# The step sizes' logarithm in the decay exponents, and a predicated copy between the two directions

## The chip, the cores and the metric

The kernel runs on one core of one Trainium2 chip. The metric is the device time of one execution in microseconds (us). A core has TensorE for matrix products (PE in the rows; its weight loads are PEld), VectorE (DVE), ScalarE (ACT), GpSimd (POOL), and SyncE (SP), whose queue issues the DMA transfers. Each engine runs its own queue in order; semaphores tie the queues together.

## The reference, cut to what matters

The model is a two-layer encoder over 512 tokens of width 1024. Layer 0 mixes tokens by retention and neighbourhood attention, layer 1 by a bidirectional state space scan; each layer ends in a gated feed-forward block. The change touches only the state space mixer of layer 1: 32 heads of width 64 in 4 groups of 8 heads, each direction with step sizes dt and decays of its own.

```python
dt = softplus(dt_raw.reshape(bsz, s, 2, SSD_HEADS) + dt_bias)
log_a = dt * -exp(a_log)
v_f = xh * dt[:, :, 0];  v_b = xh * dt[:, :, 1]
y = bidir_scan(qc, kb, v_f, v_b, log_a[:, :, 0], log_a[:, :, 1])
# within one chunk of 128 tokens and one direction:
seg = cs[:, :, None] - cs[:, None, :]            # cs = cumsum(log_a)
decay = exp(where(mask, seg, -inf))
y_intra = einsum('bjlgh,blghp->bjghp', qk[..., None] * decay, vv)   # vv = x * dt
```

Within a chunk, token j therefore gets from token l the product qk(j,l) times exp(cs(j) - cs(l)) times dt(l) times x(l), by the forward quantities where l <= j and by the backward ones elsewhere.

## The kernel before, in words

The trunk runs `mixer0`, `ffn`, `mixer1`, `ffn` in that order. Every projection is done in split precision: `mm3` (lines 86 to 88) issues three matrix products for one, on high and low parts that `split` makes (ACT cast at line 81, DVE subtraction at line 82). Weights come in 512 KB units through `wunit`, whose DMA (line 61) goes into one of three buffers `wst`.

`mixer1` first runs `steps` (lines 588 to 652). It computes dt for all 64 direction-heads over 512 tokens as 128 x 256 tiles, the running sums `pf`, the scalings `ysc` (to DRAM as `yd`) and `sw`, writes `pf` to DRAM as `pd`, and turns three tiles by PE transposes into `tok`, a token-major tile with 128 tokens on the partitions: `tok[:, 0]` holds the running sums, `tok[:, 1]` dt, `tok[:, 2]` sw. Line 652 makes `ddt`, the difference of the two directions' dt.

After that each group goes through a list of named tasks written out by hand (`SLOTS`): "t" and "n" are projections of this and the next group, "G" the 4 products of B and C per group (`gt`), "s" the chunk states, "h" one head's decay matrix, "i" the contribution of the states for a pair of heads, "p" the matrix products of a pair of heads (`py`, line 782), "r" and "o" the normalisation and output projection of the group before. This list gives the program order. The framework's scheduler then sets the order in each engine's queue when the kernel is built: by program order, by what it reckons ready, with the weight splits moved ahead by `high_priority(60)`. So a queue is not in program order throughout; but once built, it is fixed.

One head (`head`, lines 729 to 747) loads two rows of `pd`, one for each direction, broadcast to all 128 partitions (`pb`, 256 KB each, 3 buffers, line 736). Then, for each of 4 chunks, ACT computes tok minus pb for the forward direction (line 741), DVE takes the backward difference and the larger of the two (line 742), and ACT computes `ds`, which is dt forward where the mask `um` is one and dt backward elsewhere (line 744). Over the whole 128 x 512 tile follow one exponential on ACT (745), the product with `gt` on DVE (746) and the product with `ds` on DVE (747). The result is waited for by `pair`, whose 16 matrix products of a pair of heads all wait for both heads. `state` (line 717) multiplies x by rows of `tok[:, 2]`.

Of the kernel before, what the change touches and what calls it, by code (L numbers as in the profile page):

```python
# [7 lines left out]
F32 = mybir.dt.float32  # L8
R32 = mybir.dt.float32r
BF16 = mybir.dt.bfloat16  # L10
AF = mybir.ActivationFunctionType
ALU = mybir.AluOpType
PSUM = bass.MemoryType.PSUM
# [2 lines left out]
P = 128  # L16
S = 512
NT = S // P
# [517 lines left out]
SSD_H = NG * HPG  # L536
# [16 lines left out]
def mixer1(E, w_dt, w_fm, cw, dtc, cols, mask, w_out, g_post_row, done):  # L553
# [4 lines left out]
    nc, tc = E.nc, E.tc  # L558
    C = P
    H, H2 = SSD_H, 2 * SSD_H  # L560
    with ExitStack() as ctx:
        pool = lambda name, bufs: ctx.enter_context(tc.tile_pool(name=name, bufs=bufs))
        one, two, four = pool("m1", 1), pool("m1b", 2), pool("m1d", 4)
# [14 lines left out]
            nc.sync.dma_start(xd[t], E.x[:, t, :])  # L578


        tok = one.tile([P, 3, NT, H2], F32, name="tok")
        ddt = one.tile([P, NT, H], F32, name="ddt")
        etot = one.tile([P, H2, NT], F32, name="etot")
        pd = E.dram.tile([H2, S], F32, name="pd")
        yd = E.dram.tile([H2, S], F32, name="yd")
# [1 line left out]
        def steps():  # L587

            st = E.wst.tile([P, 512], F32, name="wst")
            nc.sync.dma_start(st, w_dt)  # L590
            wh = E.whi.tile([P, 512], R32, name="whi")
            wl = E.wlo.tile([P, 512], R32, name="wlo")
            E.split(wh, wl, st)
            ps = E.mm.tile([P, S], F32, name="mm")
            for k in range(KD):
                c = slice(k * H2, k * H2 + H2)
                E.mm3(ps[:H2], wh[:, c], wl[:, c], E.xh[:, k], E.xl[:, k], k == 0, k == KD - 1)
            bc = few.tile([P, 2], F32, name="bc")
            nc.sync.dma_start(bc, dtc)
            nc.scalar.activation(bc[:, 1:2], bc[:, 1:2], AF.Exp)  # L600
            nc.vector.tensor_scalar(bc[:, 1:2], bc[:, 1:2], -1.0, None, op0=ALU.mult)
            half = lambda name: E.tmp.tile([P, 256], F32, name=name, tag="tmp")
            chunks = lambda ap: ap.rearrange("p (c l) -> p c l", c=2)
            z, la, pf, tm = half("z"), half("la"), half("pf"), half("tm")
            for i in range(2):
                nc.scalar.activation(z[i * H2:i * H2 + H2], ps[:H2, i * 256:i * 256 + 256], AF.Identity,
                                     bias=bc[:H2, 0:1])
            with tc.tile_pool(name="lp", bufs=1) as lpp:
                dt = lpp.tile([P, 256], F32, name="dt")
                sw = lpp.tile([P, 256], F32, name="sw")  # L610
                ysc = lpp.tile([P, 256], F32, name="ysc")
                msk = half("msk")
                lp = log1p_exp_neg(E, lambda n: lpp.tile([P, 256], F32, name="lp_" + n), z)
                nc.vector.scalar_tensor_tensor(dt, z, 0.0, lp, op0=ALU.max, op1=ALU.add)
                nc.vector.tensor_scalar(la, dt, bc[:, 1:2], None, op0=ALU.mult)
                nc.vector.memset(msk, 1.0)
                nc.vector.memset(chunks(msk)[:, :, 0:1], 0.0)
                nc.vector.tensor_tensor_scan(pf, msk, la, 0.0, op0=ALU.mult, op1=ALU.add)
                ones = lpp.tile([P, P], F32, name="ones")
                diag = lpp.tile([P, 2, P], F32, name="diag")  # L620
                tot = lpp.tile([P, 2, 1], F32, name="tot")
                nc.vector.tensor_copy(tot, chunks(pf)[:, :, C - 1:C])
                for i in range(2):
                    r = slice(i * H2 + H, i * H2 + H2)
                    nc.vector.tensor_tensor(pf[r], pf[r], la[r], op=ALU.subtract)
                nc.vector.tensor_tensor(chunks(tm), tot.broadcast_to([P, 2, C]), chunks(pf), op=ALU.subtract)
                et = lpp.tile([P, 2], F32, name="et")
                nc.scalar.activation(et, tot.rearrange("p c o -> p (c o)"), AF.Exp)

                nc.vector.memset(ones, 1.0)  # L630
                for c in range(2):
                    nc.vector.tensor_scalar(diag[:, c], E.ident, et[:, c:c + 1], None, op0=ALU.mult)
                pe = E.px.tile([P, 2, P], F32, name="pe", tag="px")
                nc.tensor.matmul(pe.rearrange("p c n -> p (c n)"), ones, diag.rearrange("p c n -> p (c n)"),
                                 start=True, stop=True)
                nc.scalar.copy(etot.rearrange("p h (i c) -> p c i h", i=2), pe.rearrange("p c (i h) -> p c i h", i=2))
                for i in range(2):
                    r = slice(i * H2, i * H2 + H2)
                    nc.sync.dma_start(pd[:, i * 256:i * 256 + 256], pf[r])
                    f, b = slice(i * H2, i * H2 + H), slice(i * H2 + H, i * H2 + H2)  # L640
                    nc.scalar.activation(ysc[f], pf[f], AF.Exp)
                    nc.scalar.activation(ysc[b], tm[b], AF.Exp)
                    nc.scalar.activation(sw[f], tm[f], AF.Exp)
                    nc.scalar.activation(sw[b], pf[b], AF.Exp)
                    nc.sync.dma_start(yd[:, i * 256:i * 256 + 256], ysc[r])
                nc.vector.tensor_tensor(sw, sw, dt, op=ALU.mult)
                for i, s in enumerate((pf, dt, sw)):
                    pt = E.px.tile([P, 2, 2, H2], F32, name="pt", tag="px")
                    for c in range(2):
                        nc.tensor.transpose(pt[:, c].rearrange("p i h -> p (i h)"), s[:, c * C:(c + 1) * C], E.ident)  # L650
                    nc.scalar.copy(tok[:, i].rearrange("p (i c) h -> p c i h", i=2), pt)
            nc.vector.tensor_tensor(ddt, tok[:, 1, :, :H], tok[:, 1, :, H:], op=ALU.subtract)

        def rows(i, dr, g, c):
            o = dr * H + g * HPG
            return tok[:, i, c, o:o + HPG].rearrange("p (h o) -> p h o", o=1).broadcast_to([P, HPG, 64])
# [55 lines left out]
        def state(o, dr, i):  # L712

            g = o["g"]
            c = i if dr == 0 else NT - 1 - i
            xs = E.tmp.tile([P, 512], F32, name="xs", tag="tmp")
            nc.vector.tensor_tensor(hv(xs), hv(o["x"][:, c]), rows(2, dr, g, c), op=ALU.mult)
            ps = E.px.tile([P, 512], F32, name="st", tag="px")
            nc.tensor.matmul(ps, o["bt"][:, c], xs, start=True, stop=True)  # L719
            ns = one.tile([P, 512], F32, name=f"state{dr}{i}")  # L720
            if i == 0:
                nc.scalar.copy(ns, ps)
            else:
                h = dr * H + g * HPG
                nc.vector.tensor_tensor(hv(ns), hv(o["st"][dr, i - 1]), etot[:, h:h + HPG, c:c + 1].broadcast_to([P, HPG, 64]),
                                        op=ALU.mult)
                nc.vector.tensor_tensor(ns, ps, ns, op=ALU.add)
            o["st"][dr, i] = ns

        def head(o, j):  # L730

            g = o["g"]
            h = g * HPG + j
            pb = [three.tile([P, S], F32, name="pb", bufs=3) for _ in range(2)]
            for dr in range(2):
                nc.sync.dma_start(pb[dr], pd[dr * H + h].partition_broadcast(P))
            e = three.tile([P, NT, C], F32, name="e")
            ds = ys.tile([P, NT, C], F32, name="ds")
            for c in range(NT):
                cc = slice(c * C, (c + 1) * C)  # L740
                nc.scalar.activation(e[:, c], pb[0][:, cc], AF.Identity, scale=-1.0, bias=tok[:, 0, c, h:h + 1])  # L741
                nc.vector.scalar_tensor_tensor(e[:, c], pb[1][:, cc], tok[:, 0, c, H + h:H + h + 1], e[:, c],
                                               op0=ALU.subtract, op1=ALU.max)
                nc.scalar.activation(ds[:, c], um, AF.Identity, scale=ddt[:, c, h:h + 1], bias=tok[:, 1, c, H + h:H + h + 1])  # L744
            nc.scalar.activation(e, e, AF.Exp, scale=-1.0)
            nc.vector.tensor_tensor(e, e, o["gt"], op=ALU.mult)
            o["m"][j] = e, nc.vector.tensor_tensor(e, e, ds, op=ALU.mult)  # L747

        def inter(o, q):

# [228 lines left out]
def _layouts(np, i):  # L979
# [19 lines left out]
    cw = np.concatenate([i["c_conv_w"][0], i["c_conv_b"][0][None]])  # L999
    xw, bw, cw = cw[:, :2048].reshape(6, NG, 4, P), cw[:, 2048:2560].reshape(6, NG, 1, P), cw[:, 2560:].reshape(6, NG, 1, P)  # L1000
    a["c_cw"] = np.concatenate([bw, cw, xw], 2).transpose(3, 1, 2, 0)
    a["c_dtc"] = np.tile(np.stack([i["c_dt_bias"][0].reshape(-1), i["c_a_log"][0].reshape(-1)], 1), (2, 1))
    d = np.repeat(i["c_d_skip"][0].reshape(4 * NG, 2), 64, 1)
    a["c_cols"] = np.stack([d.T, i["c_norm_g"][0].reshape(4 * NG, P).T], 1)
    a["c_mask"] = np.triu(np.ones((P, P), np.float32))
# [37 lines left out]
```

## Time and profile before

| | us |
|---|---|
| median of 3 runs | 1435.91 |
| lowest, highest | 1434.77, 1436.99 |
| the profiled execution | 1435.64 |
| its span in the trace | 1433.9 |
| PE busy | 1400.5 |
| DVE busy | 945.2 |
| ACT busy | 718.4 |
| POOL busy | 61.4 |

The span is the stretch from the first to the last recorded instruction; 1.7 us of the profiled execution lie around it. Busy time counts the union of an engine's instructions. "Idle before" in the rows is time in which an engine had nothing running just before an instruction, with the event that ended it. PEclk is TensorE's granted clock as a share of full speed (1.0 is 2.4 GHz, 0.5 is 1.2 GHz).

### The profile page before, as it was taken

The page shows a single profiled execution, that of the slowest core. Times are in us where ns is not written, and L with a number is a line of the kernel's source. Part 1 is how long each engine was busy: PE and PEld are TensorE (multiplying, and loading weights), DVE is VectorE, ACT ScalarE, POOL GpSimd, SP SyncE. Part 2 cuts the span into 40 slices and gives each one's busy share as a digit, 9 for nine tenths or more (in the row PEclk, how much of TensorE's full clock was granted, in tenths as well). Part 3 has the DMA queues.
Part 4 walks back from the last instruction along what each step waited for, and adds up shares of the span by engine and source line. Part 5 has one row for each costly group of instructions (what it writes and reads, how often), then busy time and mean ns, then how long its engine had stood idle before and what let it go on. Part 6 is the DMA issues. An engine that isn't in the chain of part 4 may idle for free.

```text
span 1433.9 us, 18004 instructions
## 1 busy us (share of the span) xinstructions
PE 1400.5 (98%) x6832; PEld 1144.0 (80%) x6832; DVE 945.2 (66%) x1486; ACT 718.4 (50%) x1192; POOL 61.4 (4%) x67
## 2 busy tenths in 40 slices
PE   7999999999999999999999999999889999999998
PEld 6877777898888888888778787777678888888886
DVE  6478888666566552457789886998986666564232
ACT  4346666444444431334887866676644444443230
POOL 0010110100000000000000000000110000000000
PEclk9999999999999999999999999999999999999999
DMA  7443232232332333423565354354532333323221
GB/s 283 148 132 101 85 96 77 86 105 89 103 93 99 101 93 100 131 84 107 144 190 172 121 172 142 93 153 154 152 114 83 100 101 91 103 90 102 88 103 59
DMA packets 56950, 166.34 MB, mean 116 GB/s; under 512 B 7200, under 2 KB 7968, under 8 KB 56864
## 3 DMA queue, kind: packets, MB, share of 16 engines
q1 hardware_dynamic: 56864, 165.20, 36.4%
q8 instruction: 54, 0.88, 0.2%
q14 instruction: 32, 0.26, 0.1%
HBM read 157.57 MB, written 5.51 MB: 114 GB/s over the span
## 4 chain that ended last, share of the span: by engine, by line
PE 88%; DVE 4%; ACT 3%; DMA 2%; issue 2%; POOL 0%; SPq 0%; DVEq 0%; POOLq 0%; ACTq 0%
PE mm L86 27%; PE mm L87 26%; PE mm L88 26%; PE pi L762 1%; DMA pb<-pd 1%; PE st L719 1%; PE py L782 1%; PE pt L140 1%; PE y L449 1%; PE sc L433 1%; DVE wlo L82 0%; PE pt L663 0%; PE sc L434 0%; DMA x<-in_x 0%; ACT whi L81 0%
## 5 line engine op out<-in xcount | busy, mean ns | idle before, releaser
L88 PE MATMUL mm<-xl,whi 128*128 128x512 f32 (+2 forms) x1216 | 463.4, 381 | 3.0 <-DVE xl L82 3.0
L86 PE MATMUL mm<-xh,whi 128*128 128x512 f32 (+1 forms) x1216 | 464.5, 382 | 1.4 <-ACT bf L692 1.2
L87 PE MATMUL mm<-xh,wlo 128*128 128x512 f32 (+2 forms) x1216 | 462.8, 381 | 0.0
L82 DVE TENSOR_TENSOR wlo<-wst,whi 128x1024 fp32r<-128x1024 f32 (+1 forms) x208 | 256.0, 1231 | 125.2 <-ACT whi L81 120.6
L81 ACT CAST whi<-wst 128x1024 fp32r<-128x1024 f32 (+1 forms) x208 | 216.5, 1042 | 125.9 <-PE mm L87 96.3
L88 PEld LDWEIGHTS mm<-xl,whi 128*128 128x128 f32 (+1 forms) x1216 | 229.0, 188 | 47.2 <-DVE xl L82 3.2
L86 PEld LDWEIGHTS mm<-xh,whi 128*128 128x128 f32 x1216 | 229.2, 188 | 46.2 <-ACT bf L692 1.6
L87 PEld LDWEIGHTS mm<-xh,wlo 128*128 128x128 f32 (+1 forms) x1216 | 229.0, 188 | 42.7 <-issue 0.6
L227 DVE SCALAR_TENSOR_TENSOR cv<-mm,cwt,cv 128x511 f32<-128x511 f32 x88 | 66.0, 750 | 148.9 <-ACT cv L226 148.9
L226 ACT ACTIVATE cv<-mm,cwt 128x512 f32<-128x512 f32 x88 | 68.7, 780 | 128.0 <-PE mm L88 128.0
L86 PE MATMUL mm<-whi,hh 128*128 128x512 f32 x288 | 112.0, 389 | 0.0
L87 PE MATMUL mm<-whi,hl 128*128 128x512 f32 x288 | 112.0, 389 | 0.0
L88 PE MATMUL mm<-wlo,hh 128*128 128x512 f32 x288 | 112.0, 389 | 0.0
L81 ACT CAST hh<-cv 128x512 fp32r<-128x512 f32 x44 | 27.3, 621 | 103.3 <-DVE cv L235 103.3
L228 DVE SCALAR_TENSOR_TENSOR cv<-mm,cwt,cv 128x511 f32<-128x511 f32 x88 | 66.0, 750 | 3.0
L86 PEld LDWEIGHTS mm<-whi,hh 128*128 128x128 f32 x288 | 54.1, 188 | 11.3
L87 PEld LDWEIGHTS mm<-whi,hl 128*128 128x128 f32 x288 | 54.1, 188 | 11.2
L88 PEld LDWEIGHTS mm<-wlo,hh 128*128 128x128 f32 x288 | 54.1, 188 | 11.2
L744 ACT ACTIVATE ds<-um,tok,ddt 128x128 f32<-128x128 f32 x128 | 55.3, 486 | 11.9 <-DVE e L747 11.8
L741 ACT ACTIVATE e<-pb,tok 128x128 f32<-128x128 f32 x128 | 43.1, 392 | 16.6 <-DMA pb<-pd 14.6
L82 DVE TENSOR_TENSOR hl<-cv,hh 128x512 fp32r<-128x512 f32 x44 | 30.5, 693 | 28.9 <-ACT hh L81 28.9
L683 DVE SCALAR_TENSOR_TENSOR xf<-mm,cwt,xf 128x511 f32<-128x511 f32 (+1 forms) x64 | 47.2, 741 | 3.1 <-ACT xf L680 2.9
(236 smaller groups left out, 1932.8 us busy)
## 6 DMA issues: line engine op xcount, KB each, us to landing
wst<-in_f_up SPq DMA_DIRECT2D x88, 512.0 KB
wst<-in_f_down SPq DMA_DIRECT2D x44, 512.0 KB
wst<-in_c_fm SPq DMA_DIRECT2D x40, 512.0 KB
pb<-pd SPq DMA_DIRECT2D x64, 256.0 KB
wst<-in_ab_fm SPq DMA_DIRECT2D x20, 512.0 KB
gain<-yd SPq DMA_DIRECT2D x32, 256.0 KB
wst<-in_c_out SPq DMA_DIRECT2D x16, 512.0 KB
gain<-in_norms SPq DMA_DIRECT2D x8, 512.0 KB
```

What stands on the lines that cost most here:

```text
L81: self.nc.scalar.copy(hi, src)
L82: self.nc.vector.tensor_tensor(lo, src, hi.bitcast(F32), op=ALU.subtract)
L86: mm(out, lh, rh, start=first, stop=False)
L87: mm(out, ll, rh, start=False, stop=False)
L88: mm(out, lh, rl, start=False, stop=last)
L140: nc.tensor.transpose(pt[:, j], xs[:, j * P:(j + 1) * P], self.ident)
L226: nc.scalar.activation(o, ps, AF.Identity, scale=w(1), bias=w(3))
L227: nc.vector.scalar_tensor_tensor(o[:, 1:], ps[:, :S - 1], w(0), o[:, 1:], op0=ALU.mult, op1=ALU.add)
L228: nc.vector.scalar_tensor_tensor(o[:, :S - 1], ps[:, 1:], w(2), o[:, :S - 1], op0=ALU.mult, op1=ALU.add)
L683: nc.vector.scalar_tensor_tensor(r[:, a], ps[:, b], wc(j), r[:, a], op0=ALU.mult, op1=ALU.add)
L741: nc.scalar.activation(e[:, c], pb[0][:, cc], AF.Identity, scale=-1.0, bias=tok[:, 0, c, h:h + 1])
L744: nc.scalar.activation(ds[:, c], um, AF.Identity, scale=ddt[:, c, h:h + 1], bias=tok[:, 1, c, H + h:H + h + 1])
```

## The change

Four edits, all in `mixer1`:

- `steps` no longer turns dt into `tok` and no longer makes `ddt`. Instead it forms `ex` = sign * pf + ln(max(dt, 1e-20)), with one DVE clamp, one ACT `Ln`, and one DVE `scalar_tensor_tensor`, all on 128 x 256; the sign (-1 forward, +1 backward) is a third column of the small tile `bc`. `tok` has two parts: `ex` and `sw`.
- `head` loads the same two rows of `pd`, now into 5 buffers. ACT adds the per-token `ex` to both, direction by direction and chunk by chunk (8 instructions, backward with scale -1, in place), instead of 4 differences and 4 `ds`.
- One DVE `copy_predicated` over 128 x 512 copies the forward exponent over the backward one where `um` is not zero. It takes the place of the 4 DVE instructions with the maximum.
- The exponential reads the picked exponents; it already holds dt. So only the product with `gt` is left on DVE, and the tile `ds` is gone.

```diff
-        tok = one.tile([P, 3, NT, H2], F32, name="tok")
-        ddt = one.tile([P, NT, H], F32, name="ddt")
+        tok = one.tile([P, 2, NT, H2], F32, name="tok")
...
-            bc = few.tile([P, 2], F32, name="bc")
+            bc = few.tile([P, 3], F32, name="bc")
...
-                for i, s in enumerate((pf, dt, sw)):
+                ex = lpp.tile([P, 256], F32, name="lp_e")
+                nc.vector.tensor_scalar(ex, dt, 1e-20, None, op0=ALU.max)
+                nc.scalar.activation(ex, ex, AF.Ln)
+                nc.vector.scalar_tensor_tensor(ex, pf, bc[:, 2:3], ex, op0=ALU.mult, op1=ALU.add)
+                for i, s in enumerate((ex, sw)):
...
-            nc.vector.tensor_tensor(ddt, tok[:, 1, :, :H], tok[:, 1, :, H:], op=ALU.subtract)
...
-            nc.vector.tensor_tensor(hv(xs), hv(o["x"][:, c]), rows(2, dr, g, c), op=ALU.mult)
+            nc.vector.tensor_tensor(hv(xs), hv(o["x"][:, c]), rows(1, dr, g, c), op=ALU.mult)
...
-            pb = [three.tile([P, S], F32, name="pb", bufs=3) for _ in range(2)]
+            pb = [three.tile([P, NT, C], F32, name="pb", bufs=5) for _ in range(2)]
             for dr in range(2):
                 nc.sync.dma_start(pb[dr], pd[dr * H + h].partition_broadcast(P))
+
+            for dr in range(2):
+                for c in range(NT):
+                    nc.scalar.activation(pb[dr][:, c], pb[dr][:, c], AF.Identity, scale=1.0 - 2 * dr,
+                                         bias=tok[:, 0, c, dr * H + h:dr * H + h + 1])
+            nc.vector.copy_predicated(pb[1], um.bitcast(U32).rearrange("p (o l) -> p o l", o=1).broadcast_to([P, NT, C]), pb[0])
             e = three.tile([P, NT, C], F32, name="e")
-            ds = ys.tile([P, NT, C], F32, name="ds")
-            for c in range(NT):
-                cc = slice(c * C, (c + 1) * C)
-                nc.scalar.activation(e[:, c], pb[0][:, cc], AF.Identity, scale=-1.0, bias=tok[:, 0, c, h:h + 1])
-                nc.vector.scalar_tensor_tensor(e[:, c], pb[1][:, cc], tok[:, 0, c, H + h:H + h + 1], e[:, c],
-                                               op0=ALU.subtract, op1=ALU.max)
-                nc.scalar.activation(ds[:, c], um, AF.Identity, scale=ddt[:, c, h:h + 1], bias=tok[:, 1, c, H + h:H + h + 1])
-            nc.scalar.activation(e, e, AF.Exp, scale=-1.0)
-            nc.vector.tensor_tensor(e, e, o["gt"], op=ALU.mult)
-            o["m"][j] = e, nc.vector.tensor_tensor(e, e, ds, op=ALU.mult)
+            nc.scalar.activation(e, pb[1], AF.Exp)
+            o["m"][j] = e, nc.vector.tensor_tensor(e, e, o["gt"], op=ALU.mult)
...
-    a["c_dtc"] = np.tile(np.stack([i["c_dt_bias"][0].reshape(-1), i["c_a_log"][0].reshape(-1)], 1), (2, 1))
+    sign = np.repeat(np.array([-1, 1], np.float32), SSD_H)
+    a["c_dtc"] = np.tile(np.stack([i["c_dt_bias"][0].reshape(-1), i["c_a_log"][0].reshape(-1), sign], 1), (2, 1))
```

## Rows read from the trace of the kernel before

**Rows 1.** The profile's page: busy time, share of span and instructions by engine.

```profile
PE 1400.5 (98%) x6832; PEld 1144.0 (80%) x6832; DVE 945.2 (66%) x1486; ACT 718.4 (50%) x1192; POOL 61.4 (4%) x67
```

**Rows 2.** Busy time by stretch: start:end, length, PE, PEld, DVE, ACT, POOL, clock, DMA.

```profile
700.00:1040.00 340.00, 330.52 (x1710) 263.75 (x1709) 295.60 (x514) 245.88 (x478) 22.20 (x15) 0.98 0.49 150
```

**Rows 3.** Waits of PE, 640 to 1040 us: total, times, longest.

```profile
PE py L782 <- DVE e L747: 2.8, 1, 2.8
PE py L782 <- DVE ti L766: 2.1, 2, 1.8
PE pss L802 <- POOL sq L792: 1.4, 1, 1.4
...
PE mm L87 <- DVE yl L795: 1.1, 2, 0.6
```

**Rows 4.** Busy time by short stretches behind three waits of PE, columns as in Rows 2.

```profile
722.50:726.00 3.50, 3.50 (x26) 3.17 (x27) 2.71 (x4) 2.59 (x7) 0.00 (x0) 0.58 0.48 165
...
969.00:972.00 3.00, 3.00 (x8) 2.35 (x8) 1.79 (x2) 2.83 (x6) 0.00 (x0) 0.50 0.47 133
...
1028.00:1031.00 3.00, 2.48 (x14) 1.39 (x11) 3.00 (x3) 0.83 (x2) 2.02 (x1) 0.63 0.94 229
```

**Rows 5.** DVE by line, 700 to 1040 us: count, busy, mean ns, idle before.

```profile
L742 DVE SCALAR_TENSOR_TENSOR e<-pb,tok,e 128x128 f32<-128x128 f32 x128 | 39.1, 353 | 4.8 <-DMA pb<-pd 4.8
L747 DVE TENSOR_TENSOR e<-e,ds 128x512 f32<-128x512 f32 x32 | 21.6, 681 | 0.1
```

**Rows 6.** ACT by line, same stretch and columns.

```profile
L744 ACT ACTIVATE ds<-um,tok,ddt 128x128 f32<-128x128 f32 x128 | 55.3, 486 | 11.9 <-DVE e L747 11.8
...
L741 ACT ACTIVATE e<-pb,tok 128x128 f32<-128x128 f32 x128 | 43.1, 392 | 16.6 <-DMA pb<-pd 14.6 <-PE py L782 2.0
```

**Rows 7.** Steps, 664 to 704 us, by line: DVE rows first, then ACT rows.

```profile
L270 DVE RECIPROCAL lp_s<-lp_s 128x256 f32<-128x256 f32 x1 | 1.7, 1746 | 0.0
L276 DVE TENSOR_SCALAR lp_r<-lp_r 128x256 f32<-128x256 f32 x6 | 1.7, 288 | 0.1
...
L717 DVE TENSOR_TENSOR xs<-xt,tok 128x512 f32<-128x512 f32 x1 | 0.7, 693 | 6.0 <-ACT xt L664 6.0
...
L614 DVE SCALAR_TENSOR_TENSOR dt<-z,lp_r 128x256 f32<-128x256 f32 x1 | 0.4, 415 | 0.0
```

**Rows 8.** ACT by line, 664 to 704 us, columns as in Rows 5.

```profile
L641 ACT ACT_TABLE_LOAD x1 | 1.3, 1283 | 0.0
...
L641 ACT ACTIVATE ysc<-pf 32x256 f32<-32x256 f32 x2 | 0.8, 416 | 1.9 <-DVE pf L618 1.8
L642 ACT ACTIVATE ysc<-tm 32x256 f32<-32x256 f32 x2 | 0.8, 414 | 0.5 <-DVE tm L626 0.5
...
L268 ACT ACTIVATE lp_e<-lp_e 128x256 f32<-128x256 f32 x1 | 0.4, 406 | 0.0
```

**Rows 9.** ACT in order of time, first heads: start, length, what, idle before.

```profile
697.54 1.28 ACT L689 ACT_TABLE_LOAD   x1
698.83 0.63 ACT L689 ACTIVATE xf<-xf 128x512 f32<-128x512 f32 x1
...
704.67 1.28 ACT L741 ACTIVATE e<-pb,tok 128x128 f32<-128x128 f32 x4
...
712.85 1.28 ACT L741 ACTIVATE e<-pb,tok 128x128 f32<-128x128 f32 x4 [1.73 <-DMA pb<-pd]
...
716.59 1.15 ACT L745 ACTIVATE e<-e 128x512 f32<-128x512 f32 x2
```

**Rows 10.** SP's queue in order of time: start, length, what.

```profile
699.49 1.41 SPq L736 DMA_DIRECT2D pb<-pd  x3
...
705.98 0.32 SPq L736 DMA_DIRECT2D pb<-pd  x1
```

**Rows 11.** PE in order of time, around the steps and the first pair.

```profile
697.36 0.44 PE L650 MATMUL pt<-head,sw 128*128 128x128 f32 x2
...
722.46 1.45 PE L782 MATMUL py<-e,xt 128*64 128x128 f32 x16 [2.81 <-DVE e L747]
```

**Rows 12.** ACT in order of time ahead of PE's wait at 965 us.

```profile
958.50 0.70 ACT L741 ACTIVATE e<-pb,tok 128x128 f32<-128x128 f32 x2 [4.00 <-DMA pb<-pd]
...
960.70 3.19 ACT L744 ACTIVATE ds<-um,tok,ddt 128x128 f32<-128x128 f32 x8
...
964.39 0.62 ACT L788 ACTIVATE sq<-y 128x512 f32<-128x512 f32 x1
```

More of the change, by code (lines that the diff above doesn't have):

```diff
@@ L10 @@
 BF16 = mybir.dt.bfloat16
+U32 = mybir.dt.uint32
 AF = mybir.ActivationFunctionType
```

## The prediction

> **What bounds the kernel now.** I read the engines' shares first: PE is busy for 1400.5 of the span's 1433.9 us, DVE for 66% and ACT for 50% [rows 1]. So the most that any change off PE can give is PE's idle time plus what a lowered clock costs; a faster DVE or ACT gives nothing by itself. Then I cut out the stage that the change touches. From 700 to 1040 us PE is busy for 330.5 of 340 us, so it idles 9.5 us; DVE is busy for 295.6 (87%) and ACT for 245.9 (72%) [rows 2]. The list of PE's waits says what those 9.5 us are: 2.8 us for a head's last product, 2.1 for `ti`, 1.4 for POOL's sum of squares, 1.1 for `yl` [rows 3]. The rest is smaller or belongs to the projections' SiLU, which the change leaves alone. Last I read the clock behind these waits. It falls to its lower level for a while after PE has stood: 0.58 over 3.5 us, 0.50 over 3.0 us, 0.63 over 3.0 us [rows 4]. At full clock those stretches' work would have taken 3.5 x 0.42 = 1.5 us, 3.0 x 0.50 = 1.5 us and 3.0 x 0.37 = 1.1 us less. So the stage holds some 7.4 us of waits that heads could influence and about 4.1 us of clock behind them: 11.5 us, 0.8% of the whole. That is the ceiling.
>
> **The engines' work per head.** DVE loses four instructions of 353 ns and one of 681 ns; over 32 heads their busy time is 39.1 + 21.6 = 60.7 us [rows 5]. It gets one predicated copy of 128 x 512, an operation that no row shows. The nearest row is the two-stream TENSOR_TENSOR of that size, 681 ns [rows 5]; I take 0.68 us, since the copy too reads two streams, mask and data. Below, it can hardly undercut the 288 ns of a one-stream TENSOR_SCALAR of half the size; above, the dearest DVE row is the reciprocal, 1746 ns for 256 columns, so 3.5 us for 512 [rows 7]. With 0.68 DVE adds 21.8 us, falls by 38.9 us to 256.7 and is busy 75% of the stage. It breaks even at 60.7 / 32 = 1.90 us a copy. The Trainium skill ("VectorE: DVE Perf Modes", section on the perf-mode tier table) lets a plain fp32 copy run at twice a tensor_tensor's rate and prices no predicated one; if this one fell into the copy's tier an estimate would be 0.35 us, and the sum below would move by under 0.7 us at the first pair and nothing elsewhere.
>
> ACT loses 128 `ds` (55.3 us busy) and 128 differences (43.1) and gets 256 additions of the differences' form, a constant scale and a per-token bias [rows 6]. Four of these in a row take 1.28 us [rows 9], so 64 x 1.28 = 81.9 us in place of 98.4: ACT falls by 16.5 us to 229, 67%. But there is a shift in kind: half of ACT's old pieces (`ds`) needed no load and could run while `pb` was under way; all eight new ones sit behind `pb`, and ACT, which works in order, already stood 14.6 us for `pb` [rows 6]. Behind a waiting ACT stand the weight casts that PE needs. Against that, five buffers instead of three let the fourth load go out without waiting for a reader: before, three went out from 699.49 and the fourth only at 705.98 [rows 10]. It also shortens SP's queue, in which weight loads stand behind a `pb` that has no buffer.
>
> **The first pair (PE stands 2.81 us until 722.46).** PE is ready at 722.46 - 2.81 = 719.65 [rows 11]. On ACT, the stretch from 704.67 to the end of the first two exponentials at 717.74 is 13.1 us [rows 9]. Counted in the time-ordered view, whose first and last differences the rows show, it holds 12 differences (3.8 us), four `ds` at 0.4 each behind their overlap, and 1.73 us of waiting for a load. Now it needs 16 additions, 4 x 1.28 = 5.1 us, no `ds`, and with the earlier fourth load no such wait: 13.1 - 3.8 - 1.6 - 1.7 + 5.1 = 11.1, so about 715.8; if the third head's eight get between, 718.4. Behind it DVE has only one product of 0.68 a head instead of two. With a weight split between them the pair is ready between 717.7 and 720.3, against PE's 719.65. So the wait goes or shrinks to 0.6 us, and if it goes the clock stays up too: 2.8 + 1.5 = 4.3 us at best, nothing at worst if the additions are queued late. I take 3.3.
>
> **The wait for POOL near 965.** ACT stood 4.0 us for `pb`, then did a burst of eight `ds` (3.19 us), and only then the square that POOL and PE waited for [rows 12]. Without `ds` and with an earlier load the square comes sooner. Ends: 0 (eight additions take the burst's place, 2.6 us) and 1.4 + 1.5 = 2.9. I take half, 1.5.
>
> **The end of the mixer, 1023 to 1038.** PE waits for `ti` (2.1) and `yl` (1.1) with 1.1 of clock behind [rows 3, 4], 4.3 us. DVE is the late engine, and it now does some 9.7 us less in the last group (38.9 / 4). But part of this waits for the last projection's SiLU, which no head delays. Ends 0 and 4.3; I take 1.2.
>
> **Steps.** PE does two transposes less, 0.44 us [rows 11]; I take 0.4 saved. One clamp (0.29) and one three-operand instruction (0.42) come in on DVE, one difference and nothing else goes; they fill gaps of a dependency chain, and I cost them at nothing because the chain runs beside projections; without this cover 0.7 us. ACT gets a logarithm of 128 x 256, 0.41 us by the exponential of that size, and table loads of 1.283 us: one if the table it brings also serves the exponentials behind it, two if theirs must come back [rows 8]. That makes 1.7 to 3.0 us, against 1.9 + 0.5 = 2.4 us in which ACT stood in this stretch [rows 8]. In the holes it costs nothing; queued behind the exponentials it delays the `xt` copies, for which DVE already stood 6.0 us [rows 7], by the full 3.0. I take a loss of 1.0. Here a load and the work after it follow directly: 697.54 + 1.28 = 698.82, next start 698.83 [rows 9]. The Trainium skill ("ScalarE: Activation LUTs", section on what ACT_TABLE_LOAD costs) counts about 2.66 us for a switch, the load and a drain of 1.38, and says that exp and ln share one set; by its price two switches would be 5.3 us, and the loss here up to 5.7 instead of 3.0. The row shows the load alone, so the sum keeps 1.283.
>
> **The sum.** Gains 3.3 + 1.5 + 1.2 + 0.4 = 6.4, loss 1.0: 5.4 us. The profiled execution took 1435.64, 0.27 under the median of the runs shown, so I set the two equal: 1435.6 - 5.4 = 1430.2.
>
> **The rivals.**
> *No change (chance 0.24).* The eight additions wait for loads and take the place of the waits removed, and since PE's queue is fixed at the build, the new order brings small waits of its own elsewhere. For it: ACT's 14.6 us behind `pb`, the ceiling of 11.5 us in all. Against: two more buffers. The first pair then gains 1, steps cost 1, the rest nothing: about 1435.2.
> *Slower by the logarithm (0.15).* It is queued behind the exponentials, both tables are loaded, `xt` and so `xs` and the states come 3.0 us later. PE then stands some 3 us more before 722, with 1.5 us of clock, and the first pair's gain goes with it: 1435.6 + 3.0 + 1.5 - 0.4 = 1439.7. It decides as soon as more than 2.4 us of new ACT work stands ahead of the `xt` copies; under that the holes take it.
> *A dear predicated copy (0.04).* From 1.90 us a copy DVE has more work than before; at 3.5 us it would have 295.6 - 60.7 + 112 = 347 us of work in 340, so 7 us more than the stage holds, and 51 if its present 44 us of idle time stay; halfway between, about 1465.
> *The change doesn't lighten DVE as counted* (a copy of 1.4 us, twice a two-stream row) only shrinks the gains; it lies in the forecast's own spread.
>
> **Chances and range.** The forecast, a gain with most of the first pair's wait gone, has 0.57. Bounds: all three waits with their clock and no cost give 4.3 + 2.9 + 4.3 + 0.4 = 11.9, so 1423.7; the logarithm's rival gives 1439.7. The range 1424.5 to 1439.0 leaves out the last edge of both and the dear copy. About 0.2%, 2.9 us, is what a measurement of this kernel can tell from no change. Faster by more than that: 0.57; within: 0.25, nearly all of the second case; slower: 0.18, the logarithm and the dear copy.
>
> **What would show it.** Right: the predicated copy near 0.7 us, DVE near 257 us and ACT near 229 in the stage, the first `py` starting before 720 us with no wait for `e` and no drop of the clock behind it, fewer and shorter waits of ACT for `pb`. Wrong: a table load between the exponentials of the steps and a later first `xs`; ACT waits for `pb` above 14.6 us; a copy above 1.4 us; or PE's idle time in the stage still near 9.5 us with other names in its list of waits.

## The result, and the profile after

| | before | after |
|---|---|---|
| median of 11 runs each, us | 1434.77 | 1439.13 |
| lowest, highest | 1432.46, 1437.08 | 1436.90, 1441.03 |
| the profiled execution | 1435.64 | 1439.13 |
| its span | 1433.9 | 1437.4 |

The ratio after to before is 1.0028, with a 95% interval of 1.0019 to 1.0037: the change makes the kernel slower by some 4 us, where 5.4 us less were forecast. The two profiled spans differ by 3.5 us, so the traces hold the loss.

The busy line of the page after stands against [rows 1]; behind it come two rows of busy time by stretch (start:end, length, PE, PEld, DVE, ACT, POOL, clock, DMA), of which the first answers to [rows 2]. In the after kernel the lines of `head` are 740 (load of `pb`), 744 (the eight additions), 746 (predicated copy), 748 (exponential) and 749 (product with `gt`).

```profile
PE 1400.4 (97%) x6830; PEld 1142.5 (79%) x6830; DVE 914.4 (64%) x1359; ACT 707.1 (49%) x1193; POOL 61.1 (4%) x67
```

```profile
700.00:1040.00 340.00, 328.65 (x1702) 261.50 (x1700) 261.74 (x384) 231.42 (x474) 19.57 (x14) 0.99 0.49 150
690.00:1045.00 355.00, 342.12 (x1770) 272.21 (x1769) 271.87 (x401) 241.83 (x494) 21.00 (x15) 0.99 0.49 149
```

The same view of before, from the same start to the end of the same work:

```profile
690.00:1041.50 351.50, 342.02 (x1772) 273.17 (x1771) 302.81 (x528) 254.19 (x494) 22.20 (x15) 0.99 0.50 151
```

DVE and ACT became lighter as meant: DVE fell by 30.9 us and ACT by 12.4 in this stretch. PE's busy time is the same to 0.1 us. Its idle time grew from 351.50 - 342.02 = 9.48 us to 355.00 - 342.12 = 12.88: 3.4 of the 3.5 us. So the question is which wait of PE grew. The list of PE's waits after, 640 to 1060 us (total, times, longest), stands against [rows 3]:

```profile
PE pss L804 <- POOL sq L794: 6.2, 3, 5.3
PE py L784 <- DVE ti L768: 1.7, 2, 1.3
PE mm L87 <- ACT yh L796: 1.4, 2, 0.7
...
PE mm L87 <- DVE xf L687: 0.9, 1, 0.9
PE mm L87 <- ACT z L693: 0.7, 1, 0.7
```

The wait for a head's product (2.8 us) is gone, and one wait for POOL's sum of squares has grown from 1.4 to 5.3 us.

**Where the lead turns into a loss.** The first products of `pss`, the normalisation of a group, are a mark of how far PE has come. For the second group of heads they stand at the same place of PE's queue in both kernels, but for the two removed transposes. Their rows in the view of one tile, 870 to 890 us (count, duration min/median/max in ns, first and last start), before and then after:

```profile
L802 PE MATMUL pss<-mean,sq x8: 164/250/250, 880.2 to 880.9; 128*128 128x1 f32 x8
```

```profile
L804 PE MATMUL pss<-mean,sq x8: 164/250/250, 877.3 to 878.0; 128*128 128x1 f32 x8
```

At 877.3 the changed kernel is 2.9 us ahead. At the third group all of this goes. First come two rows of before in order of time (start, length, what, idle before), DVE's last work on `y` and PE's `pss`; ACT's rows are in [rows 12]:

```profile
962.96 0.68 DVE L786 TENSOR_TENSOR y<-y,z 128x512 f32<-128x512 f32 x1
```

```profile
966.61 1.05 PE L802 MATMUL pss<-mean,sq 128*128 128x1 f32 x8 [1.40 <-POOL sq L792]
```

Then the rows of after in the same order: DVE, ACT, POOL and PE around 960 us, and the clock behind them in the view by stretch.

```profile
957.41 0.70 DVE L788 TENSOR_TENSOR y<-y,z 128x512 f32<-128x512 f32 x1
```

```profile
956.83 1.28 ACT L744 ACTIVATE pb<-pb,tok 128x128 f32<-128x128 f32 x4 [1.28 <-DMA pb<-pd]
959.63 1.27 ACT L744 ACTIVATE pb<-pb,tok 128x128 f32<-128x128 f32 x4 [1.51 <-DMA pb<-pd]
960.81 0.76 ACT L684 ACTIVATE xf<-mm,cwt 128x512 f32<-128x512 f32 x1
961.47 1.03 ACT L82 CAST whi<-wst 128x1024 fp32r<-128x1024 f32 x1
962.40 0.63 ACT L790 ACTIVATE sq<-y 128x512 f32<-128x512 f32 x1
```

```profile
963.17 1.70 POOL L794 TENSOR_TENSOR sq<-sq 128x512 f32<-128x512 f32 x1 [19.72 <-ACT sq L790]
```

```profile
964.93 1.82 PE L804 MATMUL pss<-mean,sq 128*128 128x1 f32 x8 [5.26 <-POOL sq L794]
```

```profile
966.80:972.00 5.20, 5.20 (x13) 4.06 (x14) 2.08 (x4) 0.73 (x1) 1.02 (x1) 0.52 0.00 0
```

`y` of the group's last pair is ready at 957.41 + 0.70 = 958.11. Its square on ACT starts at 962.40, 4.3 us later, since ACT works in order and has the eight additions of the *next* group's last head queued ahead of it. They stand twice for `pb`; the first wait (1.28 us) and four additions are over when `y` comes, the second wait (1.51 us), the other four additions, a convolution and a weight cast fill the 4.3 us. PE has been free since 964.93 - 5.26 = 959.67.

In before `y` was ready at 962.96 + 0.68 = 963.64, the square came 0.75 us later (964.39, [rows 12]), and PE was free from 966.61 - 1.40 = 965.21. So `y` and PE both come 5.5 us sooner in after, and the square only 2.0; it no longer keeps up with them. Of PE's 5.5 us, some 2.5 are what is left of the lead. The other 3.0 are the order of PE's queue: 278 projection products stand between the `pss` of the second and of the third group, where before has 291, and from one product to the next PE takes 0.23 us.

After the wait its clock is at the lower level: 5.2 us at 0.52, which is 5.2 x 0.48 = 2.5 us lost, where [rows 4] show 1.5 for before.

**The ledger.** 5.26 - 1.40 = 3.9 us of wait, 1.0 of clock, and 0.8 because the eight small `pss` products took 1.82 us instead of 1.05 make a loss of 5.7 at the third group. At the end of the mixer PE idles 4.78 us from 975 us to the last `pss`, against 3.73: 1.05 more. So -2.9 + 5.7 + 1.0 = 3.8 us, less some 0.4 for two projection products that stand behind the last `pss` instead of ahead of it: 3.4, as measured between the last `pss` of both kernels (1044.7 against 1041.3).

### The profile page after: what moved, and what is told of

Its sections match the earlier page's. It is cut to its first block, busy times and chain, and to the rows that moved or that the text cites. A ratio compares the mean times of both kernels' runs of the same rounds, so it can differ in the third digit from the quotient of the medians.

```text
span 1437.4 us, 17921 instructions
## 1 busy us (share of the span) xinstructions
PE 1400.4 (97%) x6830; PEld 1142.5 (79%) x6830; DVE 914.4 (64%) x1359; ACT 707.1 (49%) x1193; POOL 61.1 (4%) x67
## 4 chain that ended last, share of the span: by engine, by line
PE 78%; DVE 8%; ACT 7%; DMA 4%; issue 2%; POOL 1%; SPq 0%; DVEq 0%; POOLq 0%; ACTq 0%
PE mm L87 24%; PE mm L89 23%; PE mm L88 23%; DMA pb<-pd 3%; ACT pb L744 2%; DVE wlo L83 1%; PE st L723 1%; ACT whi L82 1%; DVE xf L687 1%; PE pt L141 1%; PE y L450 1%; PE pi L764 1%; DVE yl L797 1%; PE sc L434 1%; PE sc L435 0%
## 5 line engine op out<-in xcount | busy, mean ns | idle before, releaser
L744 ACT ACTIVATE pb<-pb,tok 128x128 f32<-128x128 f32 x256 | 81.4, 392 | 20.9 <-DMA pb<-pd 20.6
L120 ACT ACTIVATE junk<-mm 128x512 bf16<-128x512 f32 x24 | 14.2, 593 | 66.1 <-PE mm L89 66.1
```

What stands on the lines that cost most here:

```text
L744: nc.scalar.activation(pb[dr][:, c], pb[dr][:, c], AF.Identity, scale=1.0 - 2 * dr, bias=tok[:, 0, c, dr * H + h:dr * H + h + 1])
```

## The experiments

**Theory.** ACT's queue runs too far ahead. Before, two tiles that come free late held ACT's work for a head back. The differences were written into `e`, whose five buffers come free only with the products of a pair. `ds` has two buffers, which come free only with DVE's last product (line 747), and that product needs `gt` of its own group. After, the additions stay in `pb`, `ds` is gone, and nothing ahead of the product with `gt` needs group data, so when the queues are set at build time, nearly a whole group of additions comes to stand ahead of the square that the group before still needs. Counted in the order of ACT's queue, work of the next group ahead of the last square of a group:

| | group 1 | group 2 | group 3 |
|---|---|---|---|
| before, differences, of 32 | 16 | 20 | 12 |
| before, `ds`, of 32 | 8 | 8 | 8 |
| after, additions, of 64 | 56 | 60 | 64 |
| after, exponentials, of 8 | 5 | 5 | 5 |

That is 3 to 5 heads of 8 before, and 7 to 8 after. The counts keep to the buffers: never more differences than five heads, always `ds` of two heads, and after the exponentials, which now write `e`, of five. For those ACT waits in after until PE's products free a buffer:

```profile
ACT e L748 <- PE py L784: 9.9, 3, 5.0
```

**Rivals.** More `pb` buffers put more transfers and more additions in each other's way; the dearer copy delays DVE; the logarithm delays the steps; or the place of the heads' work in ACT's queue costs the same in any kernel of this kind, so that moving it would help before as much.

In what follows, the order of the additions is changed by queueing them behind the last square of the group before:

```diff
-            nc.scalar.activation(sq, y, AF.Square)
+            o["lsq"] = nc.scalar.activation(sq, y, AF.Square)
...
+        def behind(g):
+            return tc.issue_after(gs[g - 1]["lsq"].ins) if g == NG - 1 else nullcontext()
...
-            for dr in range(2):
-                for c in range(NT):
+            with behind(g):
+                for dr in range(2):
+                    for c in range(NT):
```

### The last group's additions behind the square (this edit on after)

> The changed kernel, with ACT's additions of the last group's eight heads queued behind the square of the third group's last pair (an order on ACT only; all work stays). Theory A, the queue: PE's 5.3 us wait for POOL's sum of squares near 960 us comes from the next group's additions, which stand ahead of that square on ACT and wait for their loads. Then this wait falls under 1.5 us, the low clock behind it goes, and the kernel takes about 1434, some 5 us less than the changed kernel's 1439.1 and 0 to 2 us less than before. Theory B, the loads: five buffers put more transfers beside the weights', and late data is the cause wherever the additions stand: about 1439. Theory C, DVE's new chain (the copy in place, 0.75 us) is the cause: about 1439.

Measured: 1432.37 us, 0.9978 of before (0.9965 to 0.9991). ACT and PE in order of time:

```profile
958.24 0.62 ACT L794 ACTIVATE sq<-y 128x512 f32<-128x512 f32 x1
959.37 2.43 ACT L748 ACTIVATE pb<-pb,tok 128x128 f32<-128x128 f32 x8
```

```profile
960.34 1.05 PE L808 MATMUL pss<-mean,sq 128*128 128x1 f32 x8 [0.78 <-POOL sq L798]
```

The square comes at 958.24 instead of 962.40, the additions behind it, PE waits 0.78 us instead of 5.26, and the eight products take 1.05 us. In PE's queue `pss` stands even earlier here (273 products between the two, against 278), so that place alone does no harm. One order at one place turns the slower kernel into one that beats before, and by more than the 0 to 2 us expected: the wait was the loss.

### The same for all groups

```diff
-            return tc.issue_after(gs[g - 1]["lsq"].ins) if g == NG - 1 else nullcontext()
+            return tc.issue_after(gs[g - 1]["lsq"].ins) if g > 0 else nullcontext()
```

> As the run before, but in every group the heads' additions are queued behind the square of the last pair of the group before. Theory A: the third group's wait goes as well, and the smaller ones of the earlier groups; 1432 to 1436, unless a group's first pair now waits for heads that may no longer run ahead. Theories B and C: about 1439.

Measured: 1430.10 us, 0.9963 (0.9950 to 0.9976). Busy time by stretch, then ACT's wait for loads and PE's wait for POOL:

```profile
700.00:1040.00 340.00, 332.38 (x1741) 265.87 (x1740) 269.20 (x394) 230.28 (x477) 23.97 (x17) 1.00 0.51 152
```

```profile
ACT pb L748 <- DMA pb<-pd: 9.8, 8, 2.4
...
PE pss L808 <- POOL sq L798: 1.6, 2, 1.0
```

PE is busy for 332.4 of 340 us, more than in before and after, at full clock. ACT's wait for `pb` halves from 20.6 to 9.8 us. The gain is larger than the 5.7 us of the third group, and it begins earlier. Here is the second group's `pss`, which stands at the same place of PE's queue as in after:

```profile
L808 PE MATMUL pss<-mean,sq x8: 164/250/250, 873.6 to 874.3; 128*128 128x1 f32 x8
```

It starts 3.7 us earlier than in after (877.3). The additions of groups 2 and 3 stand in after's queue ahead of convolutions and casts too, not only of the last square. Of the 3.7 us, 0.6 are there before the mixer begins (the same product of PE starts at 639.93 us here and at 640.51 in after), and PE's idle time from 690 to 875 us explains some 2.2 (2.7 in after, 0.5 here); the rest isn't traced.

### All groups but the last

```diff
-            return tc.issue_after(gs[g - 1]["lsq"].ins) if g == NG - 1 else nullcontext()
+            return tc.issue_after(gs[g - 1]["lsq"].ins) if 0 < g < NG - 1 else nullcontext()
```

> The changed kernel with the order in the second and third group only, not in the last. Theory A: the last group's additions stand ahead of the third group's last square again, and PE's wait for POOL there is back at 3 us or more; a ratio to before of 1.000 to 1.004. If that wait does not depend on the order in the last group, about 0.997.

Measured: 1430.28 us, 0.9966 (0.9955 to 0.9977). The last group's additions aren't held, yet the wait did not come back:

```profile
961.67 1.05 PE L808 MATMUL pss<-mean,sq 128*128 128x1 f32 x8 [1.04 <-POOL sq L798]
```

This expectation missed. In this kernel's ACT queue only 20 additions of the last group stand ahead of group 3's last square, not 64. One reading is that the lead is built up from group to group, so that braking it in the first groups leaves little of it at the last; no run tests that by itself.

### The same order in before, all groups

> The kernel before, with the same order on ACT as the run that put every group's additions behind the last square of the group before (here: the differences and the ds). Theory A: before the change the ds tile, with two buffers that only the products free, kept ACT from running far ahead, so there is little to win: a ratio to before of 0.997 to 1.001. The changed kernel under the order (0.9963) then owes part of its gain to the change itself. Rival D: the order alone is worth all of it; then this too comes to 0.996.

```diff
+            return tc.issue_after(gs[g - 1]["lsq"].ins) if g > 0 else nullcontext()
...
+                with behind(g):
+                    nc.scalar.activation(e[:, c], pb[0][:, cc], AF.Identity, scale=-1.0, bias=tok[:, 0, c, h:h + 1])
...
+                with behind(g):
+                    nc.scalar.activation(ds[:, c], um, AF.Identity, scale=ddt[:, c, h:h + 1], bias=tok[:, 1, c, H + h:H + h + 1])
```

Measured: 1442.95 us, 1.0058 (1.0038 to 1.0078). PE's longest waits:

```profile
PE py L787 <- DVE e L752: 3.9, 2, 3.0
PE mm L86 <- DVE x L830: 3.2, 1, 3.2
```

The expectation (0.997 to 1.001) missed: the order by itself hurts before. PE waits 3.9 us for heads, 2.8 in before, and 3.2 for the `x` of a normalisation, 0.3 in before. The order holds back both differences and `ds` here, and why it costs this much isn't traced further. Rival D falls: the order helps the changed kernel and not before.

### Before with five buffers for `pb`

> The kernel before with 5 buffers for the loaded rows in place of 3 (to find the room, a 128-byte padding tile is left out). Theory A: ds still limits how far ACT runs ahead, so no wait of 5 us appears; the first pair's fourth load goes out earlier and its wait of 2.8 us shrinks by 1 or more: a ratio of 0.997 to 1.000. Theory B, more transfers in flight do harm: 1.001 or more.

```diff
-            pb = [three.tile([P, S], F32, name="pb", bufs=3) for _ in range(2)]
+            pb = [three.tile([P, S], F32, name="pb", bufs=5) for _ in range(2)]
...
-        few.tile([P, 32], F32, name="pad")
```

Measured: 1433.64 us, 0.9986 (0.9977 to 0.9995). PE's wait for a head's product, and two waits of ACT:

```profile
PE py L781 <- DVE e L746: 1.0, 1, 1.0
...
ACT ds L743 <- DVE e L746: 14.5, 6, 4.5
...
ACT e L740 <- DMA pb<-pd: 6.7, 6, 2.5
```

Two more buffers are worth some 2 us by themselves. They do not make ACT run ahead: 17, 20 and 16 differences of 32 stand ahead of the squares, about as in before. Where ACT no longer waits for loads (6.7 instead of 14.6 us), it waits longer for `ds` buffers (14.5 us instead of the 11.8 in [rows 6]). So the limits on the lead hold without the loads: 8 `ds` of 32 ahead of each square, as in before, and at most 20 differences, the five heads that `e` has buffers for. The change takes away both, `ds` and the writing into `e`. Which of them frees the lead isn't shown: neither before with more `ds` buffers nor after with the additions written into `e` was tried.

### After with three buffers for `pb`

> The changed kernel with 3 buffers for the loaded rows in place of 5. Theory B: the 5.3 us wait goes, about 1435, and ACT's waits for loads do not grow. Theory A: fewer of the next group's additions can run ahead, so the wait shrinks only in part, while the first pair waits again for its fourth load, 2 to 4 us with the clock: 1436 to 1441.

```diff
-            pb = [three.tile([P, NT, C], F32, name="pb", bufs=5) for _ in range(2)]
+            pb = [three.tile([P, NT, C], F32, name="pb", bufs=3) for _ in range(2)]
```

Measured: 1438.54 us, 1.0024 (1.0010 to 1.0037). PE's longest waits, and ACT's for loads:

```profile
PE mm L87 <- DVE xf L687: 4.0, 1, 4.0
PE pss L804 <- POOL sq L794: 2.4, 3, 0.9
...
PE py L784 <- DVE e L749: 1.8, 1, 1.8
...
ACT pb L744 <- DMA pb<-pd: 38.6, 33, 3.4
```

The lead shrinks (24, 40 and 28 additions of 64) and the wait near 960 us falls to 0.9, as the theory wants. But ACT now stands 38.6 us for loads with other work behind it, and PE pays 4.0 us at a convolution and 1.8 at a later head instead. The first pair starts at 718.59 us without a wait, so the wait expected there didn't come. The time is the same as that of after, for another reason.

### After with four buffers for `e`

> The changed kernel with 4 buffers in place of 5 for the finished decay tiles e, which only the pairs' products free. The queue of the changed kernel has 56, 60 and 64 additions of the next group (7 to 8 heads of 8) ahead of the last squares of the three groups; this one has 49, 52 and 48. Theory A in its finer form, that the lead itself does the harm: a little less lead, so the wait near 960 shrinks in part, 1 to 3 us less than the changed kernel. If only the order at the last square matters and not how many stand ahead, no change.

```diff
-        three, ys, last = pool("m1e", 5), pool("m1y", 2), pool("m1f", 1)
+        three, ys, last = pool("m1e", 4), pool("m1y", 2), pool("m1f", 1)
```

Measured: 1433.12 us, 0.9992 (0.9982 to 1.0001).

```profile
960.59 1.05 PE L804 MATMUL pss<-mean,sq 128*128 128x1 f32 x8 [0.81 <-POOL sq L794]
```

One buffer *less* for the decays makes the changed kernel faster: 1440.69 - 1433.12 = 7.6 us against after on the same chip. The lead falls to 49, 52 and 48 of 64, so the last group's additions reach no further than its sixth head, and the wait is 0.81 us. Four exponentials of the next group stand ahead of each last square, where after has five. So the count of `e` buffers limits how far ahead the heads can be. The gain is well above the 1 to 3 us expected, so the run supports the theory's direction and not its size, and against before it is no gain clear of noise.

### The square on POOL

> The changed kernel with the square of each group's last pair made by POOL (y times y) in place of ACT; everything else on ACT stays in its place, the next group's additions too. Theory A: the square no longer stands behind additions that wait for loads. DVE has y some 4 us before ACT comes to it in the changed kernel; POOL needs about 1.3 us twice, so PE's wait near 960 falls from 5.3 to 2 to 3 us and the low clock shortens; 2 to 4 us less than the changed kernel. If the wait comes from y being late and not from ACT's queue, it stays at 5 us and the time at the changed kernel's or above.

```diff
-            nc.scalar.activation(sq, y, AF.Square)
+            if q == 3:
+                nc.gpsimd.tensor_tensor(sq, y, y, op=ALU.mult)
+            else:
+                nc.scalar.activation(sq, y, AF.Square)
```

Measured: 1435.38 us, 1.0003 (0.9993 to 1.0012). POOL and PE in order of time, and the stretch behind the wait:

```profile
959.04 1.04 POOL L791 TENSOR_TENSOR sq<-y 128x512 f32<-128x512 f32 x1 [14.71 <-DVE y L788]
```

```profile
961.47 1.05 PE L807 MATMUL pss<-mean,sq 128*128 128x1 f32 x8 [2.11 <-POOL sq L797]
```

```profile
961.40:964.00 2.60, 2.53 (x15) 2.29 (x16) 1.48 (x2) 2.47 (x4) 0.02 (x1) 1.00 0.09 35
```

Here the additions stay about where they are (55, 60 and 60 come before the last squares), ACT still waits 19.6 us for their loads, and the square alone goes past them. PE's wait is 2.11 us, as expected, and the clock does not fall. That gives back 1440.69 - 1435.38 = 5.3 us against after on the same chip, more than the 2 to 4 expected and close to the 5.7 of the ledger. It tells the two halves of the theory apart for this wait: what costs time there is the square behind the additions, not the additions' number or their loads. It does not cover the whole gain of the order, which on this chip is 1435.38 - 1431.16 = 4.2 us larger.

### The predicated copy twice

> The changed kernel with the predicated copy done twice, 32 x 0.75 = 24 us more of DVE work in the stage, so DVE has about as much as before the change. Theory C, or any in which DVE's relief is worth something: 3 us or more above the changed kernel, 1442 or more. Theory A: DVE is not what PE waits for; within 2 us of 1439.

```diff
             nc.vector.copy_predicated(pb[1], um.bitcast(U32).rearrange("p (o l) -> p o l", o=1).broadcast_to([P, NT, C]), pb[0])
+            nc.vector.copy_predicated(pb[1], um.bitcast(U32).rearrange("p (o l) -> p o l", o=1).broadcast_to([P, NT, C]), pb[0])
```

Measured: 1440.66 us, 1.0039 (1.0025 to 1.0052), DVE busy 279.04 of 340 us.

```profile
PE mm L87 <- DVE xf L687: 5.6, 1, 5.6
PE pss L805 <- POOL sq L795: 4.5, 3, 2.4
```

Some 17 us more of work on DVE move the ratio from 1.0028 to 1.0039, and the two intervals overlap. The waits change places, one for a convolution on DVE being the longest now. The copy's price is not the cause of the loss.

### Without the logarithm

> The changed kernel without the logarithm in the steps, which leaves the exponents without it; with it go its table load and, before the exponentials, a second one. If the logarithm's place in the steps costs time (the prediction took 1.0 us, 3.0 at most), this is 1 to 3 us faster than the changed kernel. If it lies in ACT's idle time, as its trace suggests, the first states begin at the same time within 0.5 us and the total stays within 1 us: a ratio to before of 1.002 to 1.0035.

```diff
-                nc.scalar.activation(ex, ex, AF.Ln)
```

Measured: 1440.25 us, 1.0032 (1.0018 to 1.0045), with the wait for POOL in place (6.0 us in all, 4.9 the longest). The first `xs` starts at 705.86 us against 703.08 in after, but in this execution PE is 2.7 us later already at 640 us, ahead of the mixer (the same product starts at 643.18 against 640.51); so the states begin at the same time within 0.1 us, as expected. One thing of the expectation was wrong: only one table load goes with the logarithm (36 in this kernel and in before, 37 in after), since the one ahead of the exponentials is there without it. The logarithm and its table load cost nothing that can be measured; that rival falls.

### After, and the order for all groups, once more on one chip

> The changed kernel once more, beside the next run on the same chip: a ratio to before of 1.002 to 1.004.

> The changed kernel with every group's additions behind the last square of the group before, once more: a ratio to before of 0.995 to 0.9975, so some 0.7% under the changed kernel on the same chip.

Measured: 1440.69 us, 1.0036 (1.0024 to 1.0049), for after, and 1431.16 us, 0.9974 (0.9965 to 0.9984), with the order. The order is worth 9.5 us, 0.66%. A kernel with the change and this order is faster than before by 0.37% and 0.26% in the two measurements. In this second profile of after, PE's longest waits are

```profile
PE pss L804 <- POOL sq L794: 6.5, 3, 5.4
PE mm L87 <- DVE xf L687: 2.4, 1, 2.4
```

The wait for POOL is there again, with 5.4 us at its longest. The convolution's wait is larger than in the first profile (2.4 against 0.9), and the second group's `pss` starts at 879.6 instead of 877.3, though PE was 1.3 us earlier at 640 us (639.20 against 640.51). So the lead at that mark differs by some 3.7 us between two executions of one kernel, and what is read there from one pair of them is rough; the loss at the third group came in both. The kernel with the order stands at 873.5 at that mark, against 873.6 in its first profile.

## Why the prediction was wrong, step by step

**Right: the engines' work.** DVE fell to 261.7 us (256.7 forecast) and ACT to 231.4 (229). The copy took 752 ns where 0.68 us were assumed, 32 x 0.07 = 2.2 of DVE's 5.0 us. DVE and ACT of after by line, 700 to 1040 us (count, busy, mean ns, idle before):

```profile
L746 DVE COPY_PREDICATED pb<-um,pb 128x512 f32<-128x512 uint32 x32 | 24.0, 752 | 6.0 <-ACT pb L744 5.7
```

```profile
L744 ACT ACTIVATE pb<-pb,tok 128x128 f32<-128x128 f32 x256 | 81.4, 392 | 20.9 <-DMA pb<-pd 20.6
```

The 256 additions are busy for 81.4 us against 81.9 reckoned. But ACT's waits for `pb` grew from 14.6 to 20.6 us in spite of five buffers, the sign that the prediction had named as wrong.

**Right: the first pair.** SP's queue issues four loads at once, where [rows 10] show three, and the first pair starts at 719.15 without a wait (forecast 717.7 to 720.3). The clock stays at 1.00 from 690 to 730 us. Both in order of time:

```profile
698.58 1.89 SPq L740 DMA_DIRECT2D pb<-pd  x4
```

```profile
719.15 1.09 PE L784 MATMUL py<-e,xt 128*64 128x128 f32 x16
```

The whole 4.3 us came, a little over the 3.3 taken. Small new waits up to 877 us (0.9 for a convolution, 0.7 for `z`, 0.4 for `pss`) took about a third of it back.

**Steps: forecast a loss of 1.0, measured none.** ACT in order of time:

```profile
687.40 1.28 ACT L650 ACT_TABLE_LOAD   x1
688.69 0.42 ACT L650 ACTIVATE lp_e<-lp_e 128x256 f32<-128x256 f32 x1
689.13 1.28 ACT L642 ACT_TABLE_LOAD   x1
690.42 0.42 ACT L642 ACTIVATE ysc<-pf 32x256 f32<-32x256 f32 x1
```

Two table loads stand here, as in the dear case of that step, but it counted one too many: the exponentials' own load (line 641) is in [rows 8] too, in before. New are one load and the logarithm, 1.28 + 0.42 = 1.7 us, the lower end of the step's 1.7 to 3.0. They fill ACT's idle time: the exponential behind them starts at 690.42 against 690.58 before, when ACT had stood for DVE (the 1.8 us of [rows 8]). The first `xs` is at 703.08 us, 0.8 earlier than before. The holes of 2.4 us took the 1.7 us. Each ACTIVATE follows its load within 0.03 us (688.68 to 688.69, 690.41 to 690.42), and the second load follows the logarithm within 0.02 us (689.11 to 689.13), so no drain shows. The Trainium skill ("ScalarE: Activation LUTs", section on what ACT_TABLE_LOAD costs) puts a switch at about 2.66 us with a drain; these rows speak for the load alone.

**Wrong: the end of the mixer.** Forecast a gain of 1.2, measured a loss of 1.05. The step took DVE for the late engine. DVE and PE of after in order of time:

```profile
1027.17 0.69 DVE L788 TENSOR_TENSOR y<-y,z 128x512 f32<-128x512 f32 x1 [4.01 <-ACT z L693]
1027.78 0.55 DVE L768 TENSOR_TENSOR ti<-pi,gain 128x384 f32<-128x384 f32 x1
```

```profile
1028.48 1.09 PE L784 MATMUL py<-e,xt 128*64 128x128 f32 x16 [1.30 <-DVE ti L768]
```

DVE stands idle for 4.01 us until the last projection's SiLU (`z`), and `ti`, for which PE waits, is queued behind the product with `z`. A lighter DVE can't bring that forward. The prediction named this possibility and then took a gain all the same. The waits for `ti` did shrink, from 2.1 to 1.7 us; the loss comes from a wait that the step doesn't name, for ACT's `yh`, 1.4 us in after (in the list above) against this row of before, and from 0.6 us for the last `pss`:

```profile
PE mm L86 <- ACT yh L794: 0.2, 1, 0.2
```

Why `yh` is later isn't traced.

**Wrong, and the step that decided: "The wait for POOL near 965".** The prediction gave it a gain between 0 and 2.9 and took 1.5; it cost 5.7. Three things failed in it. It replaced the work that stood right ahead of the square in *before's* queue ("eight additions take the burst's place") and took the rest of that queue as given, though the change rewrites what the queue is made from; in its place 64 additions came to stand ahead of the square. It asked only how much sooner the square could come and held `y` and PE still. In before ACT kept the square only 0.75 us behind `y`, so a lighter burst had no more than that to give; in after `y` and PE came 5.5 us sooner, the square 2.0, and the wait grew from 1.40 to 5.26. And it closed the range at zero on the loss side without a reason that excludes a loss. The material was there: [rows 6] show ACT held 11.8 us by DVE's line 747 ahead of `ds` and 2.0 us by PE's `py` ahead of the differences, each a wait for a buffer. The prediction uses these rows for their busy time and for the waits for loads, and doesn't ask what those two waits held back. By the counts of the theory they were the limits on ACT's lead; which of them mattered more stays open. The no-change rival had the mechanism in its first half, additions that wait for loads, but priced it as a swap of waits that loses nothing. The slower rival was put on the logarithm, which did nothing; that its 1439.7 us lies next to the measured time is chance.

With this term at +5.7 and the end of the mixer at +1.0 in place of -1.5 and -1.2, and the first pair and the steps as measured (2.9 ahead in all at 877 us), the forecast's own sum gives 3.8 us of loss, against 3.5 in the spans.

## What to carry to other kernels

A tile with few buffers, freed late, holds back the engine that writes it; before removing it, or writing elsewhere, read the idle time that it causes, ask how far that engine will then run ahead, and which short, urgent instruction will come to stand behind the early work. A wait shrinks only by what its releaser gains over the engine that waits: if another term of the forecast brings that engine sooner, take it off. Work off the critical path that is made independent of its neighbours isn't free on an in-order engine: its loads and its waits are everybody's. Where that happens, holding the early work behind the urgent instruction can turn the loss into a gain (here 0.37% and 0.26% under before); one buffer less took the loss away.

## What the runs showed of the hardware that was not expected

The length of a single wait of PE does not tell whether its clock falls afterwards. Behind 1.40 us of waiting in before it stood at 0.50 for 3.0 us [rows 3, 4]; behind 5.26 us in after at 0.52 for 5.2 us; behind 2.11 us with the square on POOL it stayed at 1.00. What else enters was not tried.

A predicated copy of 128 x 512 fp32 with a broadcast mask took 752 ns, 10% more than the two-stream product of that size [rows 5].
